# Second product block of p moved ahead of a transpose at the first norm, p's preparation one unit earlier, and a bank-by-bank tail of three units in the last projection

## The chip, the cores and the metric

The kernel runs on one NeuronCore of a Trainium2 chip. Four engines matter here: PE (matrix multiply, which also makes transposes by multiplying with the identity), DVE (elementwise work and statistics), ACT (activations and copies) and POOL (a few small operations). SP issues most transfers and POOL some. The metric is the device time of one execution in microseconds; the time before is 1651.93 us, the median of three runs from 1651.26 to 1652.10.

## The reference

One decoder layer on 256 tokens of width 2048, in float32. What matters here is its second half:

```python
mix = token_mixers(x, ...)                       # ends with merged @ w_out
x = layer_norm(ALPHA * x + mix, ln1_g, ln1_b)    # the first norm
ffn = conv_gated_mlp(x, w_gate, w_up, conv_w, conv_b, w_down)
x = layer_norm(ALPHA * x + ffn, ln2_g, ln2_b)    # the second norm
x = x + sigmoid(x @ w_ple_gate) * (p @ w_ple_proj)   # the embedding gate
```

`x` is 256 x 2048, `p` is 256 x 256, `w_out` and `w_ple_gate` are 2048 x 2048, `w_ple_proj` is 256 x 2048. Nothing in `p @ w_ple_proj` depends on x.

## The kernel before

**Number format.** Every float32 operand of a product is held as two reduced-precision float32 pieces, `hi` (a rounded copy, made on ACT at L121) and `lo` (the rest, `raw - hi`, made on DVE). A product is then three matmuls: hi by hi, hi by lo, lo by hi. So each megabyte of weights costs ACT and DVE a conversion before PE can use it.

**Weights come in units** of 128 x 2048 float32 (1 MB). `prep` loads a unit as two halves into a ring of five `raw` buffers (SP, L237) and makes `hi` and `lo` in rings of six each. `unit()` hands the next one over and first prepares up to three ahead. Where one level of Strassen's scheme is used (`s_half`), a unit is a pair of 128-row blocks; seven products stand for eight, and `prep_s` also makes sums and differences of the weight blocks. Some of these were computed earlier and parked in DRAM; they come back as the tile `td` (SP, L196, 1 MB). Such a unit has four pieces: `b11` (half width), `b2`, `t13`, `t24`.

**Who sets the order.** A scheduler places instructions on PE, DVE and ACT by priorities and its own estimates, engine by engine; each engine then runs its list in that order. SP's list is in program order. Inside `end1` (the border behind the first norm) PE's order is written by hand.

**The output projection** `out_proj` runs in two halves of eight units (numbers 120 to 127 and 128 to 135). The first half takes the pairs in the order 0, 1, 3, 4, 5, 2, 6, 7; pairs 1, 3, 5 and 2 are Strassen units with a parked tile. Pair 2, unit 125, is the last of these. Its seven products go, in this order, to the banks p1, C00, C01 (from `b11` and `b2`) and p5, p7, p6, C10 (from `t13` and `t24`). Then `fold()` adds the shared banks to the residual `z`; its first step is a copy of bank p1 on ACT (`fold <- wo_p`). A table `mid` hangs other work on a unit: after unit number i of the half, `mid[i]()` is recorded.

**p's preparation** `ple_prep(0)` is such a piece: two loads `praw` of 512 KB into two of the five `raw` buffers (L1272), one load `pTr` (L1277), on ACT two copies `pw` and two small copies `pTs`, on DVE two subtractions `pw` (L1275) and two small `pTs` (L1280).

**The border behind the first norm** `end1`: the last two units of the second half are multiplied bank by bank (`tail_mm(t, c, i)`: token half t, column half c, unit i), so that token half 0 is finished first. `stat0` makes mean and scale, `norm0(g)` normalizes one group of 512 columns of `z` (on ACT, L1205, for g = 1; on DVE in two steps, L1196 and L1202, for the groups 0, 3, 2), `turn0(g)` transposes it on PE (four matmuls of 128, L1212, tile `ptl`) and splits it into `x1T`. The groups go in the order G = (1, 0, 3, 2). `proj(k, t)` multiplies block k of p for token half t: six matmuls of 512 at L353 into the banks `pp`. They need nothing from the norm and fill PE's time between the transposes. `put(t)` copies the result out. `phase0` starts the gate and up projections on token half 0, `phase1` on half 1.

**The embedding gate** at the end is again two halves. The second, `s_half("pg", 1, ...)`, has Strassen units for the pairs 2, 3, 4 and classic units otherwise (the last three are 281, 282, 283). Its argument `tail`, 2 before, says how many of the last units are multiplied bank by bank instead of into all four banks at once. With `fine`, the last bank C11 is first read as it is after the other units (`pre_g`, L1629), and the tail's share of it goes to two separate half-width banks 11b and 11c (L909, matmuls of 256 columns). For each bank DVE adds (L1617 or L1623), ACT takes the tanh (L1581), DVE multiplies (L1582) and adds (L1584), and SP stores (L1586).

Of the kernel before, what the change touches and what calls it, by code (L numbers as in the profile page):

```python
# [66 lines left out]
PG_S = ((), (2, 3, 4))  # L67
# [11 lines left out]
def tile_block(ctx: ExitStack, tc: tile.TileContext, wu, wfv, wpp, xT_in, x_in, pT_in, wlr,  # L79
# [25 lines left out]
    def s8(shape, dt=F32, name=None):  # L105
        return big.tile(shape, dt, tag="S8", name=name)
# [4 lines left out]
    def t2(name):  # L111
        return sm.tile([P, 512], F32, tag="t2", bufs=6, name=name)

    def mmtile(name):
        return pmm.tile([P, 512], F32, tag="mm", name=name)
# [4 lines left out]
    def copy(o, i, scale=1.0):  # L120
        return nc.scalar.activation(o, i, AF.Copy, bias=0.0, scale=scale)  # L121
# [127 lines left out]
    def unit(ahead=3):  # L249
        u = n_used[0]  # L250
        n_used[0] += 1
        while n_prep[0] < min(NU, u + ahead):
            prep()
        return ready.pop(u)
# [85 lines left out]
    def x_mm(banks, w, a, toks, first, last, cs=(0, 1), part=None):  # L340


        hi, lo = w
        for t in toks:
            ah = a[:, t * P:t * P + P]
            al = a[:, 256 + t * P:256 + t * P + P]
            for i, (x, v) in enumerate(((ah, hi), (ah, lo), (al, hi))):
                for c in cs:
                    bs = banks[t][c]
                    m = 512 // len(bs)  # L350
                    for j in range(len(bs)) if part is None else (part,):
                        o = c * 512 + j * m
                        nc.tensor.matmul(bs[j][:, 0:m], lhsT=x, rhs=v[:, o:o + m],  # L353
                                         start=first and i == 0, stop=last and i == 2)
# [432 lines left out]
    def cell(o, i):  # L787

        return o[:, i, 0:P], o[:, i, P:256]

    def s_sums(y):

        a11, a21, a12, a22 = [y[:, k, t * P:t * P + P] for k in range(2) for t in range(2)]
        v = t2("sums").rearrange("p (i t) -> p i t", t=P)
        for i, a, b, op in ((0, a21, a22, ALU.add), (2, a21, a11, ALU.subtract),
                            (1, v[:, 0], a11, ALU.subtract), (3, a12, v[:, 1], ALU.subtract)):
            nc.vector.tensor_tensor(v[:, i], a, b, op)
        return v
# [221 lines left out]
    for nh in range(2):  # L1020
        def ev_v(t, c, ps, nh=nh):
            z = vg[2 * nh + c][:, 0, t, :]
            with tc.high_priority(P_STAT):
# [3 lines left out]
               residual=False)  # L1027
# [7 lines left out]
    for nh in range(2):  # L1035
        def ev_r(t, c, ps, nh=nh):
# [3 lines left out]
            if 2 * nh + c == 0:  # L1040
# [3 lines left out]
               residual=False)  # L1044
# [187 lines left out]
    def out_proj(nh, tail, mid, end=None):  # L1232
        def cl(pair, j, t):
            if pair not in WO_C:
                return cell(mS[pair], ((0, 7), (1, 2))[j][t])
            i = WO_C.index(pair)
            a = mC[i // 2][:, i % 2 * 2 + j, :]
            return a[:, t * P:t * P + P], a[:, 256 + t * P:256 + t * P + P]

        def ev(t, c, ps):  # L1240
            zc = z1of(t, 2 * nh + c)
            with tc.high_priority(P_STAT):
                nc.vector.tensor_tensor(zc, zc, ps, ALU.add)
                if tail:
                    nc.vector.bn_stats(st1[t][:, 2 * nh + c, :], zc)

        s_half("wo", nh, OUT_ORDER[nh], WO_S[nh], cl, lambda pair, i: cell(mS[pair], i), z1of, ev,
               tail, mid, end)
# [11 lines left out]
    def load_gain(li, i):  # L1260
        g = s8([P, 2048], name=f"lnb{li}{i}")
        nc.sync.dma_start(g, lng[2 * li + i].broadcast_to([P, 2048]))
        gain[li].append(g)

    def ple_prep(half):

        w = [s8([P, 2048], F32R, name=f"pw{half}{i}") for i in range(2)]
        pt_ = s8([P, 2, 512], F32R, name=f"pTs{half}")
        pTs = [pt_[:, k, :] for k in range(2)]
        for k in range(2):  # L1270
            raw = ring.tile([P, 1024], F32, tag="raw", bufs=5, name=f"praw{half}{k}")
            nc.sync.dma_start(raw, wpp[half, :, k * 1024:k * 1024 + 1024])  # L1272
            o = slice(k * 1024, k * 1024 + 1024)
            copy(w[0][:, o], raw)
            nc.vector.tensor_tensor(w[1][:, o], raw, w[0][:, o].bitcast(F32), ALU.subtract)  # L1275
        pT = t2("pTr").rearrange("p (k t) -> p k t", t=S)
        nc.sync.dma_start(pT, pT_in)  # L1277
        for k in range(2):
            copy(pTs[k][:, 0:256], pT[:, k, :])
            nc.vector.tensor_tensor(pTs[k][:, 256:512], pT[:, k, :],  # L1280
                                    pTs[k][:, 0:256].bitcast(F32), ALU.subtract)
        return w, pTs
# [12 lines left out]
    def z1of(t, g):  # L1295
        return z1[t][:, g * 512:g * 512 + 512]
# [11 lines left out]
    pq, first = [], []  # L1308

    def end1(tail_mm):  # L1310

        x1T.extend(s8([P, 4, 512], F32R, name=f"x1T{g}") for g in range(4))
        with tc.manual_schedule(engines={mybir.EngineType.PE}):
            pb = [[[mmtile(f"pp0{t}{c}")] for c in range(2)] for t in range(2)]
            ps, us = [], []

            def proj(k, t):
                o = slice(k * 1024, k * 1024 + 1024)  # L1320
                w, pTs = pq[0]
                x_mm(pb, (w[0][:, o], w[1][:, o]), pTs[k], (t,), k == 0, k == 1)

            def put(t):
                for c in range(2):
                    o = t2("ppo")
                    tc.keep_in_program_order(copy(o, pb[t][c][0]))
                    nc.gpsimd.dma_start(ppd[t, :, c * 512:c * 512 + 512], o)

            kts = [4 * g + i for g in LN_ORDER for i in range(4)]  # L1330

            def phase0(i, part):
                if i == len(us):
                    us.append(unit())
                    ps.append(mmtile(("psg0", "psu0", "psg1")[i]))
                w_phase(ps[i], *us[i], x1T, 0, kts, part)

            def phase1(j):
                for i in range(3):
                    w_phase(ps[i], *us[i], x1T, 1, kts, slice(4 * j, 4 * j + 4))  # L1340

            for c in range(2):
                for i in range(2):
                    tail_mm(0, c, i)
            G = LN_ORDER
            (stat0, norm0, turn0), (stat1, norm1, turn1) = [
                ln_steps(z1of, st1, t, x1T, gain[0], c_g1, c_b1, "l1", P_LN1[t], AFF1[t])
                for t in range(2)]
            stat0()
            for g in G[:2]:  # L1350
                norm0(g)
            for i in range(2):
                tail_mm(1, 0, i)
            tail_mm(1, 1, 0)
            turn0(G[0])
            tail_mm(1, 1, 1)
            turn0(G[1])
            stat1()
            for g in G[2:]:
                norm0(g)  # L1360
            proj(0, 0)
            turn0(G[2])
            proj(1, 0)
            proj(0, 1)
            turn0(G[3])
            put(0)
            for g in G[:2]:
                norm1(g)
            proj(1, 1)
            for i in range(3):  # L1370
                phase0(i, slice(0, 12))
                turn1(G[i])
                if i == 0:
                    put(1)
                    for g in G[2:]:
                        norm1(g)
            for i in range(3):
                phase0(i, slice(12, 16))
            for j in range(4):
                phase1(j)  # L1380
                if j == 1:
                    turn1(G[3])
            first.extend(ps)

    def begin_out():
        for pair in (6, 7):
            turn_pair(pair)
        load_z1()

    out_proj(0, 0, {0: begin_out, 3: lambda: pq.append(ple_prep(0)),  # L1390
                    5: lambda: load_gain(0, 0)})
    out_proj(1, 2, {3: lambda: load_gain(0, 1), 4: stats1}, end1)
    mixers.append(affine(z1of, gain[0], lambda t: nc.gpsimd.dma_start(x1d[t], z1[t]), AFF1))
# [78 lines left out]
    pb, pq = [], []  # L1472
# [122 lines left out]
    def g_sums(pairs):  # L1595
        two = s8([P, 8, 256], F32R, name=f"gS{pairs[0]}")
        for i, pair in enumerate(pairs):
            o = two[:, 4 * i:4 * i + 4]
            a = x2T[pair // 2][:, pair % 2 * 2:pair % 2 * 2 + 2, :].bitcast(F32)
            y = t2("gy").rearrange("p (k t) -> p k t", t=S)  # L1600
            nc.vector.tensor_tensor(y, a[:, :, 0:256], a[:, :, 256:512], ALU.add)
            v = s_sums(y)
            copy(o[:, :, 0:P], v)
            nc.vector.tensor_tensor(o[:, :, P:256], v, o[:, :, 0:P].bitcast(F32), ALU.subtract)
            gS_[pair] = o
# [25 lines left out]
    def mid4():  # L1631
# [4 lines left out]
           begin=begin2, mid=(mid4, 4))  # L1636

    s_half("pg", 1, PG_ORDER[1], PG_S[1], g_cl, g_st, lambda t, g: zg[:, t, g - 2, :], ev_g,
           2, {0: lambda: g_sums(PG_S[1][2:])}, residual=False, fine=pre_g)
    assert n_used[0] == NU, (n_used[0], NU)  # L1640


# [103 lines left out]
```

## Time and profile before

| what | value |
|---|---|
| median of three runs | 1651.93 us (1651.26 to 1652.10) |
| the profiled execution | 1650.91 us |
| its span, first to last instruction | 1648.4 us |
| PE busy | 1639.4 us (99%) |
| DVE, ACT busy | 1336.8 us (81%), 903.3 us (55%) |
| granted PE clock | 0.999 |

The profiled execution took 2.5 us more than its span, and 1.0 us less than the median. A timeline row gives the start in us from the beginning of the span, the duration of a run of equal instructions, engine, line, operation, tiles, shape and count, and in brackets how long the engine had been idle and for whom. Two matmuls overlap: a single one is shown as 0.39 us while the next starts about 0.23 us later, so spacing is read from the starts.

### The profile page before, as it was taken

What the parts mean: (1) busy time and instruction counts of PE and PEld (TensorE: products, weight loads), DVE (VectorE), ACT (ScalarE), POOL (GpSimd) and SP (SyncE); (2) the same over time, 40 slices, a digit from 0 to 9 for tenths busy, and PEclk for the clock granted to TensorE, in tenths of its full rate; (3) what the DMA queues carried; (4) which work ended last, traced back from release to release, by engine and by line L of the source; (5) the groups of instructions that cost most, each with busy time, mean ns of one, the idle gap of its engine ahead of it and who ended that gap; (6) DMA issues with size and microseconds to landing.
All of it is one profiled execution on the core that took longest, in us unless ns stands there. A gap on an engine that the chain in (4) does not pass through costs nothing.

```text
span 1648.4 us, 23392 instructions
## 1 busy us (share of the span) xinstructions
PE 1639.4 (99%) x8429; PEld 1405.7 (85%) x8429; DVE 1336.8 (81%) x1920; ACT 903.3 (55%) x1259; POOL 89.3 (5%) x237
## 2 busy tenths in 40 slices
PE   9999999999999999999999999999999999999998
PEld 8988888888888888888888888888888888888887
DVE  7677789888888767778977888888887778989787
ACT  6755545456656654446574454555455456566554
POOL 0000000000000000000010111110111000000000
PEclk9999999999999999999999999999999999999999
DMA  9777689977878658888855898888776679899574
GB/s 324 279 262 277 227 327 343 345 251 281 292 249 283 228 194 313 304 313 308 303 185 190 315 344 319 298 301 309 277 245 216 212 260 344 299 352 341 172 261 152
DMA packets 111669, 457.35 MB, mean 277 GB/s; under 512 B 12681, under 2 KB 13969, under 8 KB 94657
## 3 DMA queue, kind: packets, MB, share of 16 engines
q1 hardware_dynamic: 103056, 404.47, 69.9%
q0 software_dynamic: 8496, 51.39, 8.0%
q8 instruction: 66, 1.08, 0.3%
q14 instruction: 51, 0.41, 0.1%
HBM read 404.42 MB, written 51.39 MB: 277 GB/s over the span
## 4 chain that ended last, share of the span: by engine, by line
PE 98%; DVE 1%; DMA 0%; ACT 0%; issue 0%; POOL 0%; SPq 0%
PE psm L973 11%; PE dn L841 10%; PE psu L307 10%; PE psg L307 9%; PE psa L973 5%; PE psu L309 5%; PE psg L309 5%; PE dn_p L841 4%; PE wo L841 3%; PE gr L841 3%; PE gv L841 3%; PE pg L353 3%; PE psb L973 3%; PE fv L472 3%; PE pg L841 2%; PE psk L307 2%
## 5 line engine op out<-in xcount | busy, mean ns | idle before, releaser
L241 DVE TENSOR_TENSOR lo<-raw,hi 128x1024 fp32r<-128x1024 f32 x466 | 564.6, 1221 | 165.6 <-ACT hi L121 163.5
L121 ACT ACTIVATE hi<-raw 128x1024 fp32r<-128x1024 f32 x466 | 488.8, 1058 | 350.4 <-DMA raw<-in_wu_dram 66.3
L307 PE MATMUL psu<-x1T,hi 128*128 128x512 f32 x688 | 240.4, 392 | 0.0
L307 PE MATMUL psg<-x1T,hi 128*128 128x512 f32 x672 | 234.9, 392 | 0.0
L309 PE MATMUL psu<-x1T,lo 128*128 128x256 f32 x688 | 192.3, 280 | 0.0
L309 PE MATMUL psg<-x1T,lo 128*128 128x256 f32 x672 | 187.9, 280 | 0.0
L973 PE MATMUL psm<-hi,xT 128*128 128x512 f32 x512 | 163.0, 392 | 0.0
L307 PEld LDWEIGHTS psu<-x1T,hi 128*128 128x128 f32 x688 | 129.2, 188 | 27.6
L307 PEld LDWEIGHTS psg<-x1T,hi 128*128 128x128 f32 x672 | 126.2, 188 | 26.9
L309 PEld LDWEIGHTS psu<-x1T,lo 128*128 128x128 f32 x688 | 130.6, 190 | 0.0
L309 PEld LDWEIGHTS psg<-x1T,lo 128*128 128x128 f32 x672 | 127.6, 190 | 0.1
L121 ACT ACTIVATE hi_b<-raw 128x512 fp32r<-128x512 f32 x102 | 85.4, 841 | 74.4 <-issue 19.1
L215 DVE TENSOR_TENSOR lo_b<-raw,hi_b 128x512 fp32r<-128x512 f32 x102 | 96.7, 954 | 35.1 <-ACT hi_b L121 34.6
L973 PEld LDWEIGHTS psm<-hi,xT 128*128 128x128 f32 x512 | 96.2, 188 | 19.6
L973 PE MATMUL psm<-lo,xT 128*128 128x512 f32 x256 | 99.7, 389 | 0.0
L159 DVE TENSOR_TENSOR td<-td 128x512 f32<-128x512 f32 x144 | 98.7, 685 | 0.6
L841 PE MATMUL dn<-hi,hC 128*128 128x512 f32 x352 | 97.8, 389 | 0.0
L215 DVE TENSOR_TENSOR lo_t<-td,hi_t 128x1024 fp32r<-128x1024 f32 x72 | 85.3, 1219 | 6.3 <-ACT hi_t L121 5.6
L121 ACT ACTIVATE hi_t<-td 128x1024 fp32r<-128x1024 f32 x72 | 75.0, 1055 | 20.4 <-DMA td<-td 6.1
L973 PE MATMUL psa<-hi,oT 128*128 128x512 f32 x256 | 81.1, 392 | 0.0
L841 PEld LDWEIGHTS dn<-hi,hC 128*128 128x128 f32 x352 | 66.0, 188 | 13.7
L121 ACT ACTIVATE hi_t<-raw 128x1024 fp32r<-128x1024 f32 x30 | 31.9, 1062 | 46.1 <-DVE raw L159 39.0
(412 smaller groups left out, 3141.1 us busy)
## 6 DMA issues: line engine op xcount, KB each, us to landing
raw<-in_wu_dram SPq DMA_DIRECT2D x532, 512.0 KB, 5.8
td<-in_wu_dram SPq DMA_DIRECT2D x36, 1024.0 KB, 8.9
td<-td POOLq DMA_DIRECT2D x36, 1024.0 KB, 6.4
td<-td SPq DMA_DIRECT2D x36, 1024.0 KB, 8.2
hS<-sd SPq DMA_DIRECT2D x11, 1024.0 KB, 9.0
raw<-in_wu_dram SPq DMA_DIRECT2D x36, 256.0 KB, 6.3
fvraw<-in_wfv_dram SPq DMA_DIRECT2D x13, 524.0 KB, 7.1
sd<-hs POOLq DMA_DIRECT2D x24, 256.0 KB, 5.8
```

Of the source, the lines that this page charges most:

```text
L121: return nc.scalar.activation(o, i, AF.Copy, bias=0.0, scale=scale)
L159: sub = lambda o, a, b: nc.vector.tensor_tensor(o, a, b, ALU.subtract)
L215: nc.vector.tensor_tensor(lo, src, hi.bitcast(F32), ALU.subtract)
L241: i = nc.vector.tensor_tensor(lo, raw, hi.bitcast(F32), ALU.subtract)
L307: nc.tensor.matmul(ps, lhsT=hi[i // 8 if hoff == 0 else 0][:, w0 % 1024:w0 % 1024 + P], rhs=a[:, kt % 4, :], start=first and i == 0, stop= ...
L309: nc.tensor.matmul(ps[:, 256:512], lhsT=lo[i // 8 if hoff == 0 else 0][:, w0 % 1024:w0 % 1024 + P], rhs=a[:, kt % 4, 0:256], start=False, ...
L353: nc.tensor.matmul(bs[j][:, 0:m], lhsT=x, rhs=v[:, o:o + m], start=first and i == 0, stop=last and i == 2)
L472: nc.tensor.matmul(fbk[t][c][:, 0:n], lhsT=x, rhs=w[:, o:o + n], start=kt == 0 and i == 0, stop=kt == 15 and i == 2)
L841: nc.tensor.matmul(ps[:, e], lhsT=x, rhs=w, start=k == 1, stop=k == total.get(id(ps), 3 * ns))
L973: nc.tensor.matmul(ps[t], lhsT=x, rhs=v, start=first and i == 0 and j == 0, stop=last and i == 3 and j == 2)
```

## The change

Three edits:

```diff
             proj(0, 0)
+            proj(1, 0)
             turn0(G[2])
-            proj(1, 0)
             proj(0, 1)
             turn0(G[3])
...
-    out_proj(0, 0, {0: begin_out, 3: lambda: pq.append(ple_prep(0)),
+    out_proj(0, 0, {0: begin_out, 2: lambda: pq.append(ple_prep(0)),
                     5: lambda: load_gain(0, 0)})
...
     s_half("pg", 1, PG_ORDER[1], PG_S[1], g_cl, g_st, lambda t, g: zg[:, t, g - 2, :], ev_g,
-           2, {0: lambda: g_sums(PG_S[1][2:])}, residual=False, fine=pre_g)
+           3, {0: lambda: g_sums(PG_S[1][2:])}, residual=False, fine=pre_g)
```

**At the border**, PE's list. The tiles `pp_7524` and `pp_7525` are the two banks of token half 0, `pp_7526` one of token half 1, `pw` and `pTs` the prepared p, `ptl` the bank of a transpose. Before, around `turn0(G[2])`:

```order
L353 MATMUL pp_7524<-pw_7062,pTs_7064 128x512
L353 MATMUL pp_7525<-pw_7062,pTs_7064 128x512
L1212 MATMUL ptl_7626<-ident,z_6865 128x128 x4
L353 MATMUL pp_7524<-pw_7062,pTs_7064 128x512
L353 MATMUL pp_7525<-pw_7062,pTs_7064 128x512
```

and now:

```order
L353 MATMUL pp_7524<-pw_7017,pTs_7018 128x512
L353 MATMUL pp_7525<-pw_7017,pTs_7018 128x512
L353 MATMUL pp_7524<-pw_7016,pTs_7018 128x512
L353 MATMUL pp_7525<-pw_7016,pTs_7018 128x512
L1212 MATMUL ptl_7632<-ident,z_6865 128x128 x4
L353 MATMUL pp_7526<-pw_7016,pTs_7018 128x512
```

Twelve matmuls of p now stand ahead of that transpose instead of six, and six instead of twelve behind it. The scheduler also reordered DVE here: the operands of the two later L1202 of token half 0 are the columns from 1024 (group 2) and then from 1536 (group 3) before, and from 1536 and then from 1024 now, so the group that `turn0(G[2])` transposes is normalized first. On ACT two weight copies moved ahead of the steps that follow the first transposes.

**In the output projection**, ACT's list around unit 125 (the pieces of unit 125, p's preparation, and the fold's copy). Before:

```order
L121 ACTIVATE hi125_b11_7022<-raw125_0_7016 128x512
L121 ACTIVATE hi125_b2_7026<-raw125_1_7017 128x1024
L121 ACTIVATE hi125_t13_7030<-td125_7020 128x1024
L121 ACTIVATE hi125_t24_7034<-td125_7020 128x1024
L121 ACTIVATE pw00_7062<-praw00_7065 128x1024
L121 ACTIVATE fold_7147<-wo0_p1_6873 128x512
L121 ACTIVATE pw00_7062<-praw01_7069 128x1024
L121 ACTIVATE pTs0_7064<-pTr_7073 128x256 x2
L121 ACTIVATE hi126_0_7081<-raw126_0_7079 128x1024
```

and now:

```order
L121 ACTIVATE pw00_7016<-praw00_7019 128x1024
L121 ACTIVATE pw00_7016<-praw01_7023 128x1024
L121 ACTIVATE pTs0_7018<-pTr_7027 128x256 x2
L121 ACTIVATE hi125_b11_7039<-raw125_0_7033 128x512
L121 ACTIVATE hi125_b2_7043<-raw125_1_7034 128x1024
L121 ACTIVATE fold_7147<-wo0_p1_6873 128x512
L121 ACTIVATE hi125_t13_7047<-td125_7037 128x1024
L121 ACTIVATE hi125_t24_7051<-td125_7037 128x1024
L121 ACTIVATE hi126_0_7081<-raw126_0_7079 128x1024
```

p's copies moved ahead of all of unit 125, and the fold's copy, which reads bank p1, now stands ahead of the two copies `t13` and `t24`. DVE's list moved in the same way, and on SP the loads of p stand ahead of the three loads of unit 125. On PE the four products from `t13` and `t24` now begin with one hi matmul each before the first lo matmul, and a few matmuls of unit 126 are mixed into them.

**At the end**, DVE's list behind the last weight conversion. `zg` is the sum of a bank, `tho` the tanh, `res` the result; `pg1_00`, `pg1_01`, `pg1_10`, `pg1_11b`, `pg1_11c` are the banks. Before, from the third bank on:

```order
L1617 TENSOR_TENSOR zg_14798<-zg_14798,pg1_10_15199 128x512
L1623 TENSOR_TENSOR zg_14798<-zg_14798,pg1_11b_15516 128x256
L1582 SCALAR_TENSOR_TENSOR tho_15510<-tho_15510,ppk1_14793 128x512
L1584 SCALAR_TENSOR_TENSOR res_15511<-tho_15510,z21_14003 128x512
L1623 TENSOR_TENSOR zg_14798<-zg_14798,pg1_11c_15517 128x256
L1582 SCALAR_TENSOR_TENSOR tho_15543<-tho_15543,ppk1_14793 128x256
L1584 SCALAR_TENSOR_TENSOR res_15544<-tho_15543,z21_14003 128x256
L1582 SCALAR_TENSOR_TENSOR tho_15550<-tho_15550,ppk1_14793 128x256
L1584 SCALAR_TENSOR_TENSOR res_15551<-tho_15550,z21_14003 128x256
```

and now:

```order
L1617 TENSOR_TENSOR zg_14798<-zg_14798,pg1_10_15199 128x512
L1582 SCALAR_TENSOR_TENSOR tho_15504<-tho_15504,ppk1_14793 128x512
L1623 TENSOR_TENSOR zg_14798<-zg_14798,pg1_11b_15510 128x256
L1584 SCALAR_TENSOR_TENSOR res_15505<-tho_15504,z21_14003 128x512
L1582 SCALAR_TENSOR_TENSOR tho_15549<-tho_15549,ppk1_14793 128x256
L1584 SCALAR_TENSOR_TENSOR res_15550<-tho_15549,z21_14003 128x256
L1623 TENSOR_TENSOR zg_14798<-zg_14798,pg1_11c_15511 128x256
L1582 SCALAR_TENSOR_TENSOR tho_15556<-tho_15556,ppk1_14793 128x256
L1584 SCALAR_TENSOR_TENSOR res_15557<-tho_15556,z21_14003 128x256
```

The two closing steps of 11b now stand ahead of the addition of 11c. On PE the tail has 18 matmuls to a bank instead of 12, the first three banks are filled side by side as the weights arrive, and the last bank has 36 matmuls of 256 columns instead of 24.

## The prediction

> **What bounds the kernel now.** I read the page's busy shares first, then the waits of PE, then the timeline of each place that the diff touches.
>
> ```profile
> span 1648.4 us, 23392 instructions
> PE 1639.4 (99%) x8429; PEld 1405.7 (85%) x8429; DVE 1336.8 (81%) x1920; ACT 903.3 (55%) x1259; POOL 89.3 (5%) x237
> ```
>
> PE is the bound from end to end. A change of order can therefore win only what PE still stands idle, or what runs behind its last matmul. The waits of PE are four in all (engine and tile, what it waited for, us in total, how often, the longest):
>
> ```profile
> PE warm_ps L131 <- DVE warm L128: 1.2, 1, 1.2
> PE ptl L1212 <- DVE z L1202: 1.0, 1, 1.0
> PE fv L472 <- ACT fvhi L121: 0.6, 1, 0.6
> PE wo L841 <- DVE lo L241: 0.6, 1, 0.6
> ```
>
> The first is the start and the third lies far from the change. The second is the border, the fourth the unit behind which p is prepared. These two and the tail are the places of the three edits, so the whole stake is some 2 to 3 us of 1650. All three sums are made against the profiled execution, 1650.91 us (2.5 us around its span of 1648.4), which lies 1.0 us under the median of 1651.93. I add the sum to the median.
>
> **The border: -1.27 us.** Its timeline before, PE first, then DVE, and a row of ACT:
>
> ```profile
> 825.58 1.64 PE L353 MATMUL pp<-pw,pTs 128*128 128x512 f32 x6
> 828.27 0.63 PE L1212 MATMUL ptl<-ident,z 128*128 128x128 f32 x4 [1.05 <-DVE z L1202]
> 828.65 2.99 PE L353 MATMUL pp<-pw,pTs 128*128 128x512 f32 x12
> 831.48 0.60 PE L1212 MATMUL ptl<-ident,z 128*128 128x128 f32 x4
> 831.83 1.64 PE L353 MATMUL pp<-pw,pTs 128*128 128x512 f32 x6
> 833.30 1.60 PE L322 MATMUL psg<-x1T,hi 128*128 128x256 f32 x12
> 826.12 0.74 DVE L1202 SCALAR_TENSOR_TENSOR z<-z,mv,lnb 128x512 f32<-128x512 f32 x1
> 827.39 0.73 DVE L1202 SCALAR_TENSOR_TENSOR z<-z,mv,lnb 128x512 f32<-128x512 f32 x1
> 828.82 0.68 DVE L1110 TENSOR_TENSOR x1T<-ptl,x1T 128x512 fp32r<-128x512 f32 x1
> 830.35 0.68 DVE L1110 TENSOR_TENSOR x1T<-ptl,x1T 128x512 fp32r<-128x512 f32 x1
> 827.46 2.01 ACT L121 ACTIVATE hi<-raw 128x1024 fp32r<-128x1024 f32 x2
> ```
>
> Six matmuls of p end their issue at 825.58 + 1.42 = 827.00; the transposes of group 3 begin at 828.27, because their L1202 is the second of the two and ends at 827.39 + 0.73 = 828.12. PE loses 1.27 us by the starts. Now twelve matmuls stand in front: by the row of twelve they take 831.48 - 828.65 = 2.83, to 828.41, and group 3 is normalized first, ready at 826.12 + 0.74 = 826.86. From there the pieces are the old ones: transposes 0.38 (828.27 to 828.65), six matmuls 1.42, the next transposes at 830.21, 0.35 more, six matmuls 1.47, so `psg` begins at 832.03 instead of 833.30.
>
> What is late next? The second transposes, at 830.21, want group 2 (now the second L1202, 828.12) and a free `ptl` bank, which the L1110 that ended at 829.50 gives: 0.71 us of slack. The last L1110 ended at 831.03 and is wanted by the last matmuls of the first `psg` group, near 833.0. But ACT's two weight copies that moved ahead (the last row, 1.0 us each) put off its copies for these steps. DVE is busy anyway until 828.1, so about one copy's length can arrive there, and 1.0 - 0.71 = 0.3 of it at PE. The bounds are -1.27, since no other idle time is there, and 0, where the wait only changes its name. I take -1.27, since the slack is shown by rows and the delay is only possible.
>
> **p's preparation: +0.25 us.** PE, then ACT and DVE around unit 125 and the beginning of unit 126:
>
> ```profile
> 766.92 0.39 PE L841 MATMUL wo_p<-hi_b,mS 128*128 128x512 f32 x1
> 768.51 0.84 PE L841 MATMUL wo_p<-hi_t,mS 128*128 128x512 f32 x3
> 771.23 1.07 PE L841 MATMUL wo<-hi,mC 128*128 128x512 f32 x4
> 772.86 0.73 PE L841 MATMUL wo<-lo,mC 128*128 128x512 f32 x2 [0.56 <-DVE lo L241]
> 762.88 2.14 ACT L121 ACTIVATE hi_t<-td 128x1024 fp32r<-128x1024 f32 x2
> 767.35 0.60 ACT L121 ACTIVATE fold<-wo_p 128x512 f32<-128x512 f32 x1 [1.39 <-PE wo_p L841]
> 767.85 1.05 ACT L121 ACTIVATE pw<-praw 128x1024 fp32r<-128x1024 f32 x1
> 768.79 0.71 ACT L121 ACTIVATE pTs<-pTr 128x256 fp32r<-128x256 f32 x2
> 764.15 2.35 DVE L215 TENSOR_TENSOR lo_t<-td,hi_t 128x1024 fp32r<-128x1024 f32 x2
> 771.58 1.22 DVE L241 TENSOR_TENSOR lo<-raw,hi 128x1024 fp32r<-128x1024 f32 x1
> ```
>
> What goes: p's copies stood in ACT's list in front of `hi126`, which so ended late, and DVE's `lo126` ended at 772.80. Four matmuls from 771.23 take 4 x 0.227 = 0.91 (the pitch is from the seven steps between 766.92 and 768.51), to 772.14; the `lo` matmul began at 772.86. PE lost 0.72. In the new list p's 2 x 1.05 + 0.71 = 2.8 us of copies run two units of work earlier, where ACT waits:
>
> ```profile
> 759.19 0.63 ACT L121 ACTIVATE hi_b<-raw 128x512 fp32r<-128x512 f32 x1 [1.66 <-PE wo L841]
> 761.91 1.06 ACT L121 ACTIVATE hi_b<-raw 128x1024 fp32r<-128x1024 f32 x1 [2.09 <-PE wo L841]
> ```
>
> These gaps, 1.66 + 2.09 us, are their cover; without it the copies would delay unit 125's own.
>
> What comes: the fold's copy now stands in ACT's list ahead of `t13` and `t24` of unit 125. It cannot begin before bank p1's last matmul (the row of 766.92; the copy followed at 767.35). The two copies, done by 765.0 before, start behind it. At the row's pitch the first runs from 767.85 to 768.91, the second from 768.82 to 769.88. PE wants the first at 768.51 and gets it at about 768.96 (0.45 lost); after two matmuls, at 769.41, it wants the second and gets it at 769.93 (0.52 lost). DVE's two subtractions of 1.2 end near 770.16 and 771.30, in front of their matmuls at 770.38 and 771.52 in the new order, and `lo126` ends near 772.46, wanted at 772.65. Lost 0.97, won 0.72: +0.25.
>
> The bounds: -0.72, if the copies come in time after all; +2.07, if PE did nothing until both subtractions are done (771.30 - 768.51 - 0.72). I take the value of the list, nearer the low end, because four `hi` matmuls and one of unit 126 stand in front of the late subtraction.
>
> The Trainium skill bears on this ("TensorE: Matmul & The Clock Gate", section "Architectural detail: the array is 16× 32×32, not 1× 128×128"): ACT and DVE are strict first-in-first-out queues, and only PE's weight loads are pulled ahead. The trace agrees: the second `pw` copy, free of any bank, stood behind the fold's copy until 767.85 while ACT idled 1.39 us. Without that rule this term would be -0.72 and the sum -2.43.
>
> The loads count too. SP's list now has p's two halves, p's transposed piece and then unit 125:
>
> ```profile
> 753.43 1.52 SPq L196 DMA_DIRECT2D td<-td  x1
> 755.04 0.86 SPq L1272 DMA_DIRECT2D praw<-in_wpp_dram  x2
> 755.94 0.58 SPq L1277 DMA_DIRECT2D pTr<-in_pT_dram  x1
> DMA to landing us min/median/max: 4.3/8.2/12.9
> ```
>
> The last row is for the parked tiles `td`. Unit 125's `td` is issued about 2.5 us later, near 755.9, and lands by the median at 764.1, by the maximum of 36 at 768.8. Its copy cannot begin before 767.85 anyway, so this costs nothing at the median and 0.95 at the maximum. DVE's and SP's other moved steps have the same answer: they run earlier, in idle time.
>
> **The tail: -0.44 us.**
>
> ```profile
> 1626.46 0.62 PE L841 MATMUL pg<-hi,x2T 128*128 128x512 f32 x2
> 1640.06 0.28 PE L909 MATMUL pg_11b<-hi,x2T 128*128 128x256 f32 x1
> 1642.81 0.28 PE L909 MATMUL pg_11c<-hi,x2T 128*128 128x256 f32 x1
> 1642.81 0.69 DVE L1584 SCALAR_TENSOR_TENSOR res<-tho,z 128x512 f32<-128x512 f32 x1
> 1643.42 0.41 DVE L1623 TENSOR_TENSOR zg<-zg,pg_11c 128x256 f32<-128x256 f32 x1
> 1644.55 0.42 DVE L1582 SCALAR_TENSOR_TENSOR tho<-tho,ppk 128x256 f32<-128x256 f32 x1
> 1645.00 0.42 DVE L1584 SCALAR_TENSOR_TENSOR res<-tho,z 128x256 f32<-128x256 f32 x1
> ```
>
> The last three units were 60 matmuls of 512 columns, 13.60 us between the first two rows, or 0.2267 each, and 24 of 256, 2.75 us over the 23 steps to the third, or 0.1196 each. With three bank by bank they are 54 and 36: 12 x 0.1196 - 6 x 0.2267 = +0.07. So the last matmul ends 0.07 later, near 1643.16. The Trainium skill (the same page, section "Back-to-back issue gap") gives N / 2.4 + 2.5 ns for an isolated warm matmul; by it the edit would cost 12 x 109 - 6 x 216 ns, +0.01. The rows are above it and decide; the difference is 0.06.
>
> Behind it, DVE added 11c at 1643.42, 0.33 after PE's end (1642.81 + 0.28 = 1643.09), since it was still at the bank before; and its L1582 waited 0.26 more behind the closing step of 11b. With those steps in front now, the sum is added at 1643.20 and the last L1584 begins at 1644.56 instead of 1645.00: -0.44, and the store behind it follows. DVE's earlier steps have 0.07 of slack at 1643.13, so little that the bounds are +0.07 (only PE's share) and -0.52 (both delays and no more matmul time).
>
> **The sum:** -1.27 + 0.25 - 0.44 = -1.46, or 1649.45 for the profiled execution and **1650.5** for the median. By the ends of the terms it runs from -2.5 to +2.1.
>
> **The rivals.**
>
> *The copies come in time (1649.5).* If the fold's copy does not hold `t13` and `t24`, or the bank is done earlier, the sum is -0.72 - 1.27 - 0.44 = -2.43. For it: they were done at 765.0 before, 3.5 us ahead of their first matmul. Against it: ACT's list, and the 1.39 us that ACT waited there.
>
> *The border's stall only moves (1651.7).* The edit then does not do what it says: the next transposes or `psg` wait for `x1T`, because ACT copies weights first. Left is +0.25 - 0.44 = -0.19. For it: DVE is full there and the order of ACT did move. Against it: 0.71 us of slack and 12 matmuls in place of the gap.
>
> *Slower, by the parked tile (1653.1).* The place is ACT in front of unit 125. `td` comes behind p's 1.25 MB now. If it lands at X, after 767.85, the loss of 0.97 grows by X - 767.85. The kernel is slower from a loss of 0.72 + 1.27 + 0.44 = 2.43 on, so from X = 769.3, 13.4 us after the issue. At 14.6 us it is 770.5: 0.97 + 2.65 - 2.43 = +1.19. For it: `td` is the largest load and its issue alone took 1.52. Against it: none of 36 took more than 12.9.
>
> **How the numbers follow.** Forecast 0.60; copies in time 0.12; stall only moves 0.13; slower 0.12; unseen 0.03. The runs before spread by 0.8 us. The range is 1648.9 to 1653.2: the second case less 0.6 of run spread, and the slower case as far as its price. The forecast's own range is 1649.7 to 1651.2. A change under 0.2% (3.3 us) can hardly be told from none; it would need 1648.6 or 1655.2. No sum of the terms reaches either. I leave 0.07 for faster and 0.08 for slower, as what no row here shows, and 0.85 for within.
>
> **What would show it.** Border: no wait at L1212 for L1202, and twelve `pp` matmuls before the second transposes; a wait at L1212 or `psg` for `x1T` or `ptl` would show the third case. Unit 125: no wait for `lo126`, but two of about 0.4 and 0.5 at `wo_p` for `hi_t`, with the fold's copy directly ahead of `hi_t` on ACT; `hi_t` waiting for the load `td` would show the slower case. Tail: the add of 11c within 0.15 us of PE's end, and PE's end at most 0.1 later against the tail's start. The prediction is wrong if PE idles more than 1.5 us around unit 125, or if a wait appears where no edit is.

## The result, and the profile after

| | before | changed |
|---|---|---|
| median of 22 runs each | 1651.46 us | 1649.34 us |
| lowest to highest | 1650.91 to 1653.14 | 1648.75 to 1650.66 |
| the profiled execution, and its span | 1650.91, 1648.4 | 1648.75, 1646.8 |

The ratio is 0.9988, with an interval of 0.9983 to 0.9994: 2.1 us faster (1.0 to 2.8 by the interval), where 1.46 was forecast. The gain is under 0.2%, as expected, and the time lies inside the range of 1648.9 to 1653.2. But it is 1.1 us under the forecast (1651.93 - 1.46 = 1650.47), under the forecast's own range of 1649.7 to 1651.2, and nearest to the 1649.5 of *the copies come in time*. The traces below show that it was not that case. Of the 1.1 us, 0.47 is the kernel before, whose median is 1651.46 over 22 runs and was 1651.93 over three; the rest is a larger gain.

The waits of PE in the changed kernel (engine and tile, what it waited for, us in total, times, the longest):

```profile
PE warm_ps L131 <- DVE warm L128: 1.2, 1, 1.2
PE wo_p L841 <- ACT hi_t L121: 0.5, 2, 0.3
```

The waits at `ptl` (1.0) and for `lo` (0.6) are gone, and one for `hi_t` at unit 125 is new, as forecast. That the wait at `fv` (0.6) is gone too is no merit of the change: it lies in the first 13 us and comes and goes from run to run. It was 0.6 us before and in experiment 3, 0.3 in experiments 7, 8 and 10, and absent in the other traces.

The timeline around unit 125, ACT, then the load of the parked tile, then PE:

```profile
762.24 1.06 ACT L121 ACTIVATE hi_b<-raw 128x1024 fp32r<-128x1024 f32 x1 [1.75 <-DMA raw<-in_wu_dram]
767.28 0.60 ACT L121 ACTIVATE fold<-wo_p 128x512 f32<-128x512 f32 x1 [3.98 <-PE wo_p L841]
767.78 2.00 ACT L121 ACTIVATE hi_t<-td 128x1024 fp32r<-128x1024 f32 x2
...
755.56 0.43 SPq L196 DMA_DIRECT2D td<-td  x1
...
766.40 0.39 PE L841 MATMUL wo_p<-hi_b,mS 128*128 128x512 f32 x1
768.22 0.39 PE L841 MATMUL wo<-hi_b,mS 128*128 128x512 f32 x1
768.88 0.73 PE L841 MATMUL wo_p<-hi_t,mS 128*128 128x512 f32 x2 [0.27 <-ACT hi_t L121]
769.83 0.50 PE L841 MATMUL wo_p<-hi_t,mS 128*128 128x512 f32 x1 [0.21 <-ACT hi_t L121]
...
770.16 0.39 PE L841 MATMUL wo<-hi_t,mS 128*128 128x512 f32 x1
...
772.68 0.62 PE L841 MATMUL wo<-lo,mC 128*128 128x512 f32 x2
```

ACT finished `b2` at 763.30 and then stood 3.98 us before the fold's copy, which waited for bank p1. The two copies of the parked tile ran straight behind it. The tile itself was there: its load took 9.1 us from its issue, so it had landed at 764.7. PE should have begun the first product of `t13` at 768.22 + 0.23 = 768.45 and began at 768.88 (0.43 lost); two matmuls later it lost 0.50 more. At unit 126 the `lo` matmuls follow without a wait.

The border, PE and DVE:

```profile
825.72 3.02 PE L353 MATMUL pp<-pw,pTs 128*128 128x512 f32 x12
828.57 0.60 PE L1212 MATMUL ptl<-ident,z 128*128 128x128 f32 x4
828.93 1.65 PE L353 MATMUL pp<-pw,pTs 128*128 128x512 f32 x6
830.41 0.60 PE L1212 MATMUL ptl<-ident,z 128*128 128x128 f32 x4
830.76 1.64 PE L353 MATMUL pp<-pw,pTs 128*128 128x512 f32 x6
832.24 1.59 PE L322 MATMUL psg<-x1T,hi 128*128 128x256 f32 x12
...
826.27 0.74 DVE L1202 SCALAR_TENSOR_TENSOR z<-z,mv,lnb 128x512 f32<-128x512 f32 x1
827.54 0.73 DVE L1202 SCALAR_TENSOR_TENSOR z<-z,mv,lnb 128x512 f32<-128x512 f32 x1
```

No bracket is left: from the first `pp` matmul to `psg` it is 6.52 us instead of 7.72. And the tail:

```profile
1625.35 0.39 PE L841 MATMUL pg<-hi,x2T 128*128 128x512 f32 x1
...
1641.78 0.28 PE L909 MATMUL pg_11c<-hi,x2T 128*128 128x256 f32 x1
...
1641.58 0.42 DVE L1584 SCALAR_TENSOR_TENSOR res<-tho,z 128x256 f32<-128x256 f32 x1
1642.10 0.42 DVE L1623 TENSOR_TENSOR zg<-zg,pg_11c 128x256 f32<-128x256 f32 x1
1643.00 0.43 DVE L1582 SCALAR_TENSOR_TENSOR tho<-tho,ppk 128x256 f32<-128x256 f32 x1 [0.48 <-ACT tho L1581]
1643.46 0.42 DVE L1584 SCALAR_TENSOR_TENSOR res<-tho,z 128x256 f32<-128x256 f32 x1
```

The addition of 11c begins 0.04 us behind PE's end (1641.78 + 0.28) instead of 0.33, and nothing stands in front of the two closing steps. From the first matmul of the last three units (1626.46 before, 1625.35 now) to the last matmul it is 16.43 us instead of 16.35: +0.08, where +0.07 was worked out. All 14 traces of this document have the one figure or the other, by their tail. Between the fixed points of the two traces (starts of instructions; the L628 matmul is a product of the token mixers and serves only as a mark) the difference divides so:

| stretch | before | changed | difference | forecast |
|---|---|---|---|---|
| start to the first L628 matmul | 101.72 | 101.67 | -0.05 | 0 |
| to bank p1's first matmul of unit 125 | 664.75 | 664.73 | -0.02 | 0 |
| to the first `pp` | 59.11 | 59.32 | +0.21 | +0.25 |
| to `psg` | 7.72 | 6.52 | -1.20 | -1.27 |
| to the last matmul | 809.51 | 809.54 | +0.03 | +0.07 |
| to the last L1584 | 2.19 | 1.68 | -0.51 | -0.51 |
| sum | 1645.00 | 1643.46 | -1.54 | -1.46 |
| from there to the span's end | 3.4 | 3.4 | 0.0 | 0 |
| outside the span | 2.5 | 1.9 | -0.6 | 0 |

The last row is the surprise: the time that lies around the span fell too. It is the execution's time less its span (1650.91 - 1648.40 and 1648.75 - 1646.85).

### The profile page after: what moved, and what is told of

The parts are those of the page before. It is cut to its first block, busy times and chain, and to the rows that moved or that the text cites. A ratio compares the mean times of both kernels' runs of the same rounds, so it can differ in the third digit from the quotient of the medians.

```text
span 1646.8 us, 23403 instructions
## 1 busy us (share of the span) xinstructions
PE 1640.1 (100%) x8435; PEld 1406.8 (85%) x8435; DVE 1336.8 (81%) x1920; ACT 903.3 (55%) x1259; POOL 89.0 (5%) x237
## 4 chain that ended last, share of the span: by engine, by line
PE 99%; ACT 0%; DVE 0%; issue 0%; POOL 0%; ACTq 0%
PE psm L973 11%; PE dn L841 10%; PE psu L307 10%; PE psg L307 9%; PE psa L973 5%; PE psu L309 5%; PE psg L309 5%; PE dn_p L841 4%; PE wo L841 4%; PE gr L841 3%; PE gv L841 3%; PE fv L472 3%; PE pg L353 3%; PE psb L973 3%; PE psk L307 2%; PE psq L307 2%
## 5 line engine op out<-in xcount | busy, mean ns | idle before, releaser
L309 PE MATMUL psu<-x1T,lo 128*128 128x256 f32 x688 | 192.3, 280 | 0.0
L309 PE MATMUL psg<-x1T,lo 128*128 128x256 f32 x672 | 187.8, 280 | 0.0
L309 PEld LDWEIGHTS psu<-x1T,lo 128*128 128x128 f32 x688 | 130.6, 190 | 0.0
L309 PEld LDWEIGHTS psg<-x1T,lo 128*128 128x128 f32 x672 | 127.6, 190 | 0.0
```

Source lines behind the costliest of these rows:

```text
L309: nc.tensor.matmul(ps[:, 256:512], lhsT=lo[i // 8 if hoff == 0 else 0][:, w0 % 1024:w0 % 1024 + P], rhs=a[:, kt % 4, 0:256], start=False, ...
```

## The experiments

Each of the twelve was timed in eleven runs beside 32 or 33 runs of the kernel before on the same chip (medians 1651.38 to 1651.48 us); the first four ran on one chip, the other eight on another. Some intervals touch 1, so a verdict rests on the stretches in the traces and the time stands beside them.

**1. The border edit alone.**

```diff
             proj(0, 0)
-            turn0(G[2])
             proj(1, 0)
+            turn0(G[2])
             proj(0, 1)
```

> Only the border edit: twelve matmuls of p ahead of the transposes of group 3; p's preparation and the tail as before. In this kernel DVE still normalizes group 2 before group 3. Theory A (one wait, which two edits remove each by itself): the twelve matmuls alone cover it, since they end 2.83 us after 825.58, at 828.41, and group 3 was ready at 828.12 to 828.27; PE's wait at L1212 is gone, psg begins 1.2 to 1.3 us earlier, and the time is 1.2 to 1.3 us under the kernel before. Theory B (the order of the two normalizations is what removed the wait, the matmuls alone do not): the wait at L1212 stays at some 1 us and the time is within 0.3 us of before. In both, the wait for lo at unit 126 (0.56) stays, and the tail is as before.

1650.12 us, 1.28 under before (ratio 0.9993, 0.9984 to 1.0002). Its timeline at the border:

```profile
825.89 3.00 PE L353 MATMUL pp<-pw,pTs 128*128 128x512 f32 x12
828.73 0.60 PE L1212 MATMUL ptl<-ident,z 128*128 128x128 f32 x4
...
832.39 1.59 PE L322 MATMUL psg<-x1T,hi 128*128 128x256 f32 x12
...
827.70 0.74 DVE L1202 SCALAR_TENSOR_TENSOR z<-z,mv,lnb 128x512 f32<-128x512 f32 x1
```

Group 3 is here the second L1202 in DVE's list, as before, ready at 828.44, and the transposes begin at 828.73 without a wait: 6.50 us to `psg`. Twelve matmuls cover the old order of DVE too, with 0.29 to spare. Theory A holds.

**2. p's preparation alone.**

```diff
-    out_proj(0, 0, {0: begin_out, 3: lambda: pq.append(ple_prep(0)),
+    out_proj(0, 0, {0: begin_out, 2: lambda: pq.append(ple_prep(0)),
```

> Only p's preparation a unit forward; six matmuls of p ahead of the transposes, tail of two units. In this kernel DVE normalizes group 3 before group 2, as in the whole change. Theory A (one wait, which two edits remove each by itself): the six matmuls end their issue 1.42 us after their start and group 3 is ready then, so the wait at L1212 is under 0.15 us and psg comes 1.1 to 1.3 us earlier against the first transposes; at unit 125 PE loses 0.93 by hi_t and no longer 0.72 by lo, +0.2; together 0.9 to 1.1 us under before. Theory B (the edits add up, each with its own wait): the wait at L1212 stays at 1.0, and the time is 0.2 us over before. If the loss at unit 125 came from the parked tile's landing and not from the fold's copy, hi_t would be released by the load in the rows.

1649.93 us, 1.47 under before (0.9991, 0.9982 to 1.0):

```profile
826.54 1.64 PE L353 MATMUL pp<-pw,pTs 128*128 128x512 f32 x6
828.02 0.60 PE L1212 MATMUL ptl<-ident,z 128*128 128x128 f32 x4
...
833.03 1.00 PE L322 MATMUL psg<-x1T,hi 128*128 128x256 f32 x7
...
827.10 0.74 DVE L1202 SCALAR_TENSOR_TENSOR z<-z,mv,lnb 128x512 f32<-128x512 f32 x1
828.37 0.73 DVE L1202 SCALAR_TENSOR_TENSOR z<-z,mv,lnb 128x512 f32<-128x512 f32 x1
```

PE still has only six matmuls ahead of the transposes, but group 3 is now the first L1202, ready at 827.84, while the six end their issue at 826.54 + 1.42 = 827.96. The transposes begin at 828.02, ahead of the second L1202. The wait is gone, 6.49 us to `psg`. So the same wait is removed a second time, by another edit, 60 us ahead of it: with p's preparation moved, the scheduler orders DVE's work at the border the other way round. How it comes to that is not shown. From p1 to `pp` it is 59.31, the +0.2 of unit 125. Theory A holds; the time fell by 0.4 more than it said, and outside the span the median fell by 0.37.

**3. The tail alone.**

```diff
-           2, {0: lambda: g_sums(PG_S[1][2:])}, residual=False, fine=pre_g)
+           3, {0: lambda: g_sums(PG_S[1][2:])}, residual=False, fine=pre_g)
```

> Only the tail of three units. By the sum: PE's end +0.07 against the tail's start, the last L1584 0.44 earlier against before, the waits at L1212 (1.0) and for lo at unit 126 (0.6) as before; the span is 0.4 to 0.5 us under that of before. The time outside the span was 2.5 us in the one profile of before and 1.9 in those of the change. Theory C (that share hangs on the end of the program, which only this edit changes): 1.9 here, and the time is about 1.0 us under before. Theory D (it hangs on something else): 2.4 to 2.5 here, and the time is about 0.4 us under before.

1650.39 us, 1.01 under before (0.9994, 0.9985 to 1.0002). Last matmul to last L1584: 1.68 instead of 2.19. The median span fell by 0.6, and outside the span are 1.90 us instead of 2.40 (medians). The number of theory C came; its reason did not survive, as the runs with p's preparation moved and the old tail (experiments 2 and 8) have 2.03 and 2.07.

**4. Border and tail without p's preparation** (the edits of 1 and 3).

> Border and tail edits without p's preparation. Theory A: the wait at L1212 is gone, the wait for lo at unit 126 (0.56, 0.72 by the starts) stays, the loss at unit 125 is gone; so the span is 1.6 to 1.8 us under before and 0.1 to 0.3 us under the whole change: moving p's preparation is a small loss once the border is mended in another way. Theory B (p's preparation brings the reordering of DVE that the border needs): the wait at L1212 stays at some 1 us and the time is 0.4 to 0.6 us under before, 1 us over the whole change.

1649.51 us, 1.89 under before (0.9988, 0.9979 to 0.9997). The first L628 matmul to `psg` takes 730.34 us, against 730.57 in the whole change and 731.58 before, so up to there the forecast 0.2 is shown. The times do not show it: 0.17 over the whole change. The profiled run lost 0.4 to a wait of L309 for `lo` behind `psg`, one of those that come and go. Theory B falls; whether p's preparation costs 0.2 in the time stays undecided. The median span is 1.5 us under before, a little less than the 1.6 to 1.8 expected.

**5. The whole change, with the fold's copy kept behind.**

```diff
-            copy(u, p1)
+            (tc.keep_in_program_order if nm == "wo" and nh == 0 else id)(copy(u, p1))
```

> The whole change with the copy of the first fold of the output projection kept in program order on ACT: it then stands behind t13 and t24 of unit 125 and behind the copies of units 126 and half of 127; PE's list is that of the whole change. Theory A (the fold's copy at the head of ACT's list is what makes hi_t late at unit 125): both waits of PE for hi_t (0.27 and 0.21 in the rows, 0.93 by the starts) are gone, bank p1 to first pp is 59.1 - 0.7 = 58.4 us instead of 59.3, and the time is 0.8 to 1.0 us under the whole change. Rival (p's loads in front of unit 125 make its parked tile td late, the fold's copy only hides that): ACT's copy of td is released by the load and not by the list, PE still waits for hi_t or lo_t, and the time is within 0.3 us of the whole change. If the later fold makes DVE or a bank late, a new wait shows behind unit 126 and the gain is given back.

1648.23 us, 3.15 under before (0.9983, 0.9974 to 0.9992). ACT and PE at unit 125:

```profile
765.31 2.01 ACT L121 ACTIVATE hi_t<-td 128x1024 fp32r<-128x1024 f32 x2 [1.40 <-DMA td<-td]
767.22 3.00 ACT L121 ACTIVATE hi<-raw 128x1024 fp32r<-128x1024 f32 x3
771.64 0.58 ACT L121 ACTIVATE fold<-wo_p 128x512 f32<-128x512 f32 x1
...
768.99 0.84 PE L841 MATMUL wo_p<-hi_t,mS 128*128 128x512 f32 x3
```

PE has no wait left but the first. With PE's list the same, p1 to `pp` is 58.25 us instead of 59.32. DVE's list changed with the edit too (`lo` of unit 127 stands ahead of the fold's steps now), but what PE had waited for was `hi_t`, and ACT makes that. The rival was right in one thing: ACT now waits for the parked tile, until 765.31. But that is 3.7 us ahead of the first product, and with both copies done by 767.32 nothing on PE is late.

**6. p's preparation a unit later** (edits 1 and 3, and `4:` in place of `3:`).

> Border and tail edits, with p's preparation moved the other way: one unit later than before instead of one earlier. In this kernel ACT copies t13 and t24 of unit 125 and both halves of unit 126 ahead of the fold's copy, and p's copies stand behind the fold. Theory A (both losses at this place are orders in ACT's list): neither the wait for hi_t nor the wait for lo at unit 126 is left; bank p1 to first pp is 58.4 us instead of 59.1 before and 59.3 in the whole change; the time is 0.7 us under the kernel with border and tail alone and 0.9 under the whole change. Rival (p's copies only move the lateness to the next unit): a wait for lo of unit 127 or for z at the fold, 58.8 us or more, and the time within 0.3 us of border and tail alone.

1650.60 us, 0.78 under before (0.9995, 0.9986 to 1.0004), and 1.1 over experiment 4. The rival holds in kind, since the lateness moves; but it moves to another place than it said, and it costs more than its 0.3 us. The wait for `lo` at unit 126 is gone, but PE meets a longer one twelve us on (PE, then DVE):

```profile
785.17 0.73 PE L841 MATMUL wo<-lo,mC 128*128 128x512 f32 x2 [1.59 <-DVE lo L241]
...
772.05 1.22 DVE L1275 TENSOR_TENSOR pw<-praw,pw 128x1024 fp32r<-128x1024 f32 x1
773.18 0.68 DVE L865 SCALAR_TENSOR_TENSOR z<-z,fold 128x512 f32<-128x512 f32 x1
773.78 1.22 DVE L1275 TENSOR_TENSOR pw<-praw,pw 128x1024 fp32r<-128x1024 f32 x1
...
779.77 0.69 DVE L865 SCALAR_TENSOR_TENSOR z<-z,fold 128x512 f32<-128x512 f32 x1
780.89 1.29 DVE L1243 TENSOR_TENSOR z<-z,wo 128x512 f32<-128x512 f32 x2 [0.43 <-PE wo L841]
782.10 0.68 DVE L866 TENSOR_TENSOR fold<-fold,wo_p 128x512 f32<-128x512 f32 x1
782.69 0.68 DVE L1243 TENSOR_TENSOR z<-z,wo 128x512 f32<-128x512 f32 x1
783.29 0.69 DVE L865 SCALAR_TENSOR_TENSOR z<-z,fold 128x512 f32<-128x512 f32 x1
783.89 1.22 DVE L241 TENSOR_TENSOR lo<-raw,hi 128x1024 fp32r<-128x1024 f32 x1
785.03 0.68 DVE L1243 TENSOR_TENSOR z<-z,wo 128x512 f32<-128x512 f32 x1
785.63 1.22 DVE L241 TENSOR_TENSOR lo<-raw,hi 128x1024 fp32r<-128x1024 f32 x1
```

And in experiment 4, DVE at the same place:

```profile
779.12 0.69 DVE L865 SCALAR_TENSOR_TENSOR z<-z,fold 128x512 f32<-128x512 f32 x1
...
780.57 0.69 DVE L865 SCALAR_TENSOR_TENSOR z<-z,fold 128x512 f32<-128x512 f32 x1
781.18 1.22 DVE L241 TENSOR_TENSOR lo<-raw,hi 128x1024 fp32r<-128x1024 f32 x1
782.32 2.47 DVE L1243 TENSOR_TENSOR z<-z,wo 128x512 f32<-128x512 f32 x4
```

p's subtractions stand in experiment 6 among the fold's steps on DVE (772.05 to 775.00). That fits the smaller part of the delay: the fold's L865 of 779.77 comes 1.0 us later than that of 779.12 (the L628 matmul starts 0.32 earlier here). The larger part is again an order in DVE's list. Three of the additions L1243, which need PE's last banks, stand ahead of the fold's end and of the `lo`; in experiment 4 all four stand behind both. So the fold is not done before 783.98 instead of 781.26, and the `lo` behind it (of unit 128), which ends at 785.11, is what PE waits for. p1 to `pp` is 60.15, 1.0 more than before.

**7. p's preparation two units forward** (the whole change with `1:` in place of `2:`).

> The whole change with p's preparation two units forward instead of one. Unit 125's load of its parked tile then no longer has p's loads right in front of it, but ACT's list still has the fold's copy ahead of t13 and t24 of unit 125. Theory A (list order): the same two waits for hi_t, 0.9 us by the starts, bank p1 to first pp 59.3 us, and the time within 0.3 us of the whole change. Rival (late loads): the waits are gone and the time is 0.7 to 0.9 us under the whole change.

1649.56 us, 1.82 under before (0.999, 0.9981 to 0.9999). The same two waits for `hi_t`, 0.5 in all, though p's loads were issued from 737.98 to 745.56, far from unit 125's. The first L628 matmul to `psg` takes 730.57 us, exactly as in the whole change. That is what the list order says. But the theory of late loads is not tested here as it was meant to be, since the parked tile's own load was issued no earlier (756.36, against 755.56 in the whole change). What it falls by is experiment 5, and the tile's landing at 764.7 in the whole change. (The stretch from p1 to `pp` can't be compared: the scheduler starts bank p1 earlier.)

**8. Border and p's preparation, old tail** (edits 1 and 2).

> The border edit together with p's preparation a unit forward, tail of two units as before. Theory A (both edits remove the same wait): from bank p1 to psg it is as long as with p's preparation alone, within 0.1 us (65.8 us), and the time is within 0.3 us of that kernel: on top of the one edit the other is worth nothing. Theory B (the edits add up): 1.2 us under p's preparation alone. The time outside the span: about 2.0 if it belongs to p's preparation as well as to the tail, 2.4 if the tail alone lowers it.

1650.10 us, 1.28 under before (0.9992, 0.9983 to 1.0). The first L628 matmul to `psg`:

| | six matmuls ahead | twelve ahead |
|---|---|---|
| p's preparation as before | 731.58 | 730.33 |
| a unit forward | 730.54 | 730.57 |

Each edit is worth 1.0 to 1.25 us alone; on top of the other, the border edit is worth nothing (+0.03) and p's preparation costs 0.24. Theory A holds.

**9 and 10. The time outside the span.**

```diff
-    for _ in range(8):
-        nc.tensor.matmul(pw_, lhsT=warm[:, 0:P], rhs=warm, start=True, stop=True)
+    for i in range(14):
+        nc.tensor.matmul(pw_[:, :512 if i < 8 else 16], lhsT=warm[:, 0:P], rhs=warm[:, :512 if i < 8 else 16], start=True, stop=True)
```

> The kernel before with six more matmuls of 16 columns on PE at the very start, behind the eight warming ones, so that PE's program is six matmuls longer, as with the tail of three units; end and border are those of before. PE awaits its first data there, so the span should be that of before within 0.3 us (waits at L1212 and for lo at unit 126 as before). Theory L (the time outside the span hangs on the length of PE's program): 1.9 to 2.0 us instead of 2.4. Theory T (it hangs on what the end of the program does): 2.4 as before.

```diff
-    nc.gpsimd.memset(mhalf, -0.5)
+    nc.gpsimd.memset(mhalf, -0.5); nc.gpsimd.memset(mhalf, -0.5); nc.gpsimd.memset(mhalf, -0.5)
```

> The kernel before with two more writes of a 128x1 tile on POOL at the start; nothing else moves on any engine. Theory L: if the length of any engine's program shifts the time outside the span, it leaves 2.4 here; if only PE's counts, it stays. Theory T: 2.4, and the time within 0.3 us of before.

1651.40 and 1651.24 us, no change (ratios 1.0 and 0.9999, each 0.0009 either way); outside the span 2.42 and 2.44. Theory L falls for additions at the start of the program.

**11 and 12. The whole change and experiment 5 side by side.**

> The whole change unaltered, beside the next kernel on the same chip: 2.0 to 2.2 us under before, span 1.6 to 1.8 under, 1.9 outside.

> The kernel with the fold's copy behind, once more, beside the whole change on the same chip. Theory A: 0.9 to 1.1 us under the whole change, no wait of PE for hi_t or lo at units 125 and 126. Rival (its first time was a lucky chip): within 0.3 us of the whole change.

1649.41 us (2.07 under before; 0.9988, 0.9979 to 0.9997) and 1648.54 us (2.94 under; 0.9981, 0.9972 to 0.999). The fold's copy behind is worth 0.87 us here, side by side, where 0.9 to 1.1 was expected. At its first time it was 1.11 under the change's 22 runs, or 1.03 when each is taken against the kernel before beside it. It is the best version found: some 3 us under before.

## Why the prediction was right, and where it was not

**What bounds.** Right: PE was busy for 1639 to 1641 us in every variant, and all that was won inside the span lay in its waits and behind its last matmul.

**The border.** The size held: -1.20 against -1.27. The next waits stayed covered: the 0.3 us that ACT's two moved copies might have given back did not arrive, since 6.52 us here is as short as the 6.50 of experiment 1, where ACT's copies did not move. (The two that moved are not both in the row shown for them: they are the copy of 825.51 and the first of the two of 827.46. The delay of about one copy's length is right all the same: the step of 826.46 came at 827.55, 1.0 us later against the first `pp` matmul.) What I had not seen is which edit does it. I put "group 3 is normalized first" down beside the twelve matmuls as one edit. Experiments 1 and 2 show two covers for one wait, and DVE's order belongs to p's preparation. For the sum it made no difference; but a forecast for p's preparation alone, made by my terms, would have been +0.25, and it came out at -1.04 in the trace.

**p's preparation.** Right in mechanism and size: +0.21 against +0.25, with 0.43 and 0.50 lost where 0.45 and 0.52 were worked out. Measured against the 58.25 us of experiment 5, where nothing waits, the stretch lost 0.86 before and 1.07 in the change, each about 0.1 more than the terms 0.72 and 0.97. The matmul behind a wait follows later than at the usual 0.23 (769.83 to 770.16 is 0.33); the two surpluses cancel in the difference, which was luck. The fold's copy in ACT's list is the cause (experiment 5 puts it behind and the loss goes), not the parked tile's landing (764.7 in the change, and no hindrance in experiment 5 either). The Trainium skill's rule that ACT takes its queue strictly in order ("TensorE: Matmul & The Clock Gate", section "Architectural detail: the array is 16× 32×32, not 1× 128×128") is borne out by the 3.98 us that ACT stood in front of the fold's copy with the two others behind it, their tile landed for the last 2.6 of them.

**The tail.** Right: +0.08 for the tail's own matmuls and -0.51 behind them, against +0.07 and -0.51. The +0.03 of the table is no measure of this, since it spans 809 us; the same kernel gave 809.54 and, in experiment 11, 809.64.

**What the sum left out.** It took the frame as fixed: it was made against the profiled execution, "2.5 us around its span of 1648.4", and I carried those 2.5 over unchanged. They became 1.9. By medians of the span the change is worth 1649.1 - 1647.4 = 1.7 us, and outside the span 2.40 - 1.92 = 0.48, together 2.2, where 2.1 was measured. The term was not mis-sized but absent, and without it the gain would have been much nearer the forecast. The runs have:

| outside the span, medians of 11 to 33 runs | us |
|---|---|
| before; border alone; experiments 9 and 10 | 2.40 to 2.44 |
| p's preparation forward, old tail (2, 8) | 2.03, 2.07 |
| tail of three (3, 4, 5, 7, 11, 12, the change) | 1.88 to 1.95 |
| tail of three, p's preparation later (6) | 2.09 |

It is neither the tail alone nor the number of instructions at the start. In the kernel before, single runs have 2.0 as well as 2.5.

The traces show where this time lies. These are the DMA transfers behind the end of the span, in the kernel before and then in the changed one:

```profile
q14 instruction: 1, 0.01, 0.3%
...
DMA packets 0, 0.00 MB, mean 0 GB/s; under 512 B 0, under 2 KB 0, under 8 KB 0
```

`q14` is a queue that the page lists with the kind `instruction`. In the kernel before, one packet of 8 KB on it starts 2.25 us behind the last instruction and ends at 2.76, and 2.51 us lie outside the span. Six of the 14 traces have such a packet (before, experiments 1, 2, 6, 8 and 9); in each the time outside the span is the packet's end less 0.24 us, from 1.90 to 2.51. The eight others have none, and 1.86 to 2.02. So in the two executions compared above, the 0.6 us goes with this packet. What decides whether it comes, and how late, stays open: the one trace of experiment 10 has none, though its runs have a median of 2.44, and no experiment removes the packet alone.

**The rivals.** *The copies come in time* did not happen in the change, but experiment 5 brought it about. It gained 0.87 and 1.11 us on the change in time and 1.07 in the stretch from p1 to `pp`, where the forecast had priced 0.97. *The stall only moves* did not happen at the border; a stall that moves is what experiment 6 shows, at the fold. *Slower, by the parked tile* was far off: in experiment 5 its copy began 3.7 us before its first product.

## What to carry to other kernels

Where a scheduler orders the work, look at what an edit does to the lists far from it: here one edit removed a wait 60 us later by an order that nobody wrote, and two edits together were worth no more than one. A copy that waits for a late bank should not stand at the head of an in-order list with ready work behind it; to find such a place, look for an engine that idles while the next engine waits for the instruction behind it. And a gain of a tenth of a percent is better read between fixed points of the traces than from one span or one time.

## What the runs showed that was not expected

The beginning of the program varies by as much as the largest edit is worth. The first L628 matmul starts at 101.72 us before, 101.67 in the change, 102.88 in experiment 3 and between 101.92 and 102.52 in the others, though nothing ahead of it was changed (but in 9 and 10). The same kernel has 101.67 in the change and 102.27 in experiment 11. From there to bank p1 it takes 664.72 to 664.75 us in 13 of the 14 traces (in experiment 7 the scheduler starts bank p1 earlier), so the scatter up to there is made in the first 100 us. Behind the border it comes back: `psg` to the last matmul took 809.47 us in experiment 2 and 811.08 in experiment 7, where PE waited 0.8 for a `lo` and 0.2 for a `hi`.
